# A two-layer trunk in float32: the residual stream kept feature-major instead of token-major

## The chip, the cores and the metric

One core of one Trainium2 chip runs the whole kernel in one launch. The metric is the device time of that launch in microseconds, median of three runs. Before the change they are 2691.78, 2687.07 and 2688.96 us, so the median is 2688.96 us.

## The reference, cut to what matters

The input is x (1024 tokens x 1024 features) with a conditioning vector c. Two layers, each a mixer and a feed-forward (hidden 2816), each wrapped the same way:

```
def rms_norm(x, g):
    y = x * lax.rsqrt(jnp.mean(x * x, axis=-1, keepdims=True) + EPS)
    return y * g
def modulate(h, shift, scale):
    return h * (1.0 + scale[:, None, :]) + shift[:, None, :]
...
    for layer in range(DEPTH):
        mod = silu(c) @ ada_w[layer] + ada_b[layer]
        sh1, sc1, g1, sh2, sc2, g2 = jnp.split(mod, 6, axis=-1)
        h = modulate(rms_norm(x, ln_mix_g[layer]), sh1, sc1)
        mix = even_mixer(h, ...) if layer % 2 == 0 else odd_mixer(h, ...)
        x = x + g1[:, None, :] * mix
        h = modulate(rms_norm(x, ln_ffn_g[layer]), sh2, sc2)
        x = x + g2[:, None, :] * swiglu(h, ffn_w_in[layer], ffn_w_out[layer])
```

The even mixer is chunked attention (A) beside a state space model (S5, whose input is u, a quarter of the input projection); the odd mixer is retention (C) beside stick-breaking attention (D). The statistics of the norm go over the features of one token; shift, scale and gate are one number for each feature.

## The kernel before, in words

T is 1024 tokens in NT = 8 tiles of 128, D is 1024 features in NK = 8 tiles of 128, the hidden layer is NH = 22 tiles taken in 11 blocks of FB = 2. Every float32 operand of a large product is split into two parts (hi and lo), and a product is three matmuls (mm3, L236 to L238). The weights come as one stream of units: a DMA into a raw tile, a copy to hi on ScalarE (L129), a subtraction to lo on GpSimd (L130; during the projections of A on VectorE). These whl and wo splits run ahead of their use.

The normalized, modulated activations stand feature-major in HT (feature on the partition, token along the row), as hi and lo. The residual x is token-major: x[t] holds 128 tokens. `rstd` squares a token tile on ScalarE with a running sum (L311) and takes the power -1/2 on GpSimd (L312 to L314); `norm` scales the rows on VectorE (xn, L323), turns eight 128x128 pieces on TensorE (L331), modulates on ScalarE (L334), and splits on VectorE (L336, L337).

In `out_proj` and in `ffn`'s outp the activations (HT, or aT, the gated hidden layer) are the stationary operand, the weights move, and a result is 128 tokens x 512 features in PSUM (banks mm, at and av). VectorE multiplies it by the gate (L1223, L1293), which has to lie along the row: so adaLN's parts 2 and 5 are broadcast over the partitions by a matmul with ones (L290) and a DMA of ada_b. GpSimd then adds the product into x (L1224, L1294); in the last block of a feed-forward VectorE adds. Other adaLN parts become columns by eight one-column matmuls (L297).

`first` starts the program: x comes in by tiles, `sums` on VectorE makes adaLN's weighted sums for the shift and scale of feature tile k (L368 to L371, eight per tile), `cols` reduces them to columns on TensorE (L378), `turn` transposes and normalizes at once by a matmul against a diagonal (dg, L407; L388), and the u projection (192 matmuls of 512 columns, five of eight token phases beside the loop) runs as feature tiles come in. After it the projections of A begin (a_dense, matmuls of 256 columns).

The order on each engine is set by a list scheduler on a simulated timeline, within what the code's steps (pipe.tick) allow: generators such as norm and ada give out a part at each step. Engines take their rows in order; a row whose input is late holds all rows behind it on its engine.

Of the kernel before, what the change touches and what calls it, by code (L numbers as in the profile page):

```python
# [30 lines left out]
class Split:  # L31
    """A float32 operand as the exact sum of two float32r parts."""
# [8 lines left out]
class Pipe:  # L41
    """Issues pieces of work in steps: a piece is a generator that yields how many steps to wait for its next part."""
# [25 lines left out]
class Unit:  # L68
    """One slot of the weight stream: [P, n] of a source, split on chip."""
# [20 lines left out]
class Stream:  # L90
    """All weights in the order of their use: loads run ahead, then the split into float32r parts."""
# [66 lines left out]
class Trunk:  # L158
    def __init__(self, ctx, tc, I, out):
# [16 lines left out]
        for name, shape in (("mixd", [NK, P, T]), ("cad", [P, 16, 2, P]), ("m2d", [P, 16, 2, P]), ("ed", [P, 16, 2, P]),  # L176
                            ("m1d", [P, 32, P]), ("kd", [16, 32, 16, 16]), ("ytd", [4, P, T]), ("vd", [8, P, NT, 64]),
                            ("qkd", [4, 2, 2, P, T]), ("xd", [T, D]), ("ud", [8, P, 512])):
            setattr(self, name, self.dr.tile(shape, F32, name=name))
        self.r8 = self.const.tile([P, 16], F32, name="r8")  # L180
        self.col, self.gbc, self.state, self.pp = {}, {}, None, None
# [4 lines left out]
    def plan(self):  # L186
        """the weights in the order of their use"""
# [52 lines left out]
    def project(self, ps, w, n, cols, ks=range(NK)):  # L240
        """token-major projection of the token columns cols, feature tiles ks"""
# [63 lines left out]
    def rstd(self, pool, xs):  # L305
        """1 / rms over the columns of the views xs [P, 4, P]"""
        nc = self.nc
        ss = self.sm.tile([P, 4], F32, tag="ss", bufs=4, name="ss")
        for h, x in enumerate(xs):
            f = pool.tile([P, 4, P], F32, tag="hf", bufs=2, name="hf")  # L310
            nc.scalar.activation(f, x, AF.Square, accum_out=ss[:, h:h + 1])  # L311
        nc.gpsimd.tensor_add(ss[:, 2:3], ss[:, 0:1], ss[:, 1:2])  # L312
        nc.gpsimd.tensor_scalar(ss[:, 2:3], ss[:, 2:3], 1.0 / D, EPS, M, A)
        nc.gpsimd.tensor_tensor(ss[:, 3:4], ss[:, 2:3], self.mhalf, ALU.pow)  # L314
        return ss[:, 3:4]

    def norm(self, pool, xt, t, sb):
        nc = self.nc
        s, b = (self.col[z] for z in sb)
        r = self.rstd(pool, [xt[:, h * 512:h * 512 + 512].rearrange("p (a b) -> p a b", a=4) for h in range(2)])  # L320
        yield 1
        xn = pool.tile([P, D], F32, tag="ada", bufs=1, name="xn")
        nc.vector.tensor_scalar(xn, xt, r, None, M)  # L323
        yield 1
        tok = slice(t * P, (t + 1) * P)
        for h in range(2):
            ps = self.at_bank()
            f = pool.tile([P, 4, P], F32, tag="hf", bufs=2, name="hf")
            for j in range(4):
                k = 4 * h + j  # L330
                nc.tensor.transpose(ps[:, j * P:(j + 1) * P], xn[:, k * P:(k + 1) * P], self.ident)  # L331
            for j in range(4):
                k = 4 * h + j
                nc.scalar.activation(f[:, j], ps[:, j * P:(j + 1) * P], AF.Identity, bias=b[:, k:k + 1], scale=s[:, k:k + 1])  # L334
            hi = self.HT.hi[:, 4 * h:4 * h + 4, tok]
            nc.vector.tensor_copy(hi, f)  # L336
            nc.vector.tensor_sub(self.HT.lo[:, 4 * h:4 * h + 4, tok], f, hi.bitcast(F32))  # L337

# [1 line left out]
    def first(self, keep, xp):  # L340
        """norm, modulation and the projection of u, feature tile by feature tile as adaLN's columns come in;
        ud[b][c, g, (s h')] = u of the groups 4 b + g at token 8 c + s"""
        nc, I, v, pipe = self.nc, self.I, self.nc.vector, self.pipe
        U = xp.tile([P, 32, 8, 16], F32, name="U")
        xs = xp.tile([P, NT, NK, P], F32, name="xs")
        dg = xp.tile([P, NT, P], F32, name="dg")
        uf = U.rearrange("p g s h -> p (g s h)")
        ax = xp.tile([P, 2048], F32, name="ax")
        slot = lambda k: ax if k % 3 == 2 else uf[:, k % 3 * 2048:k % 3 * 2048 + 2048]
# [9 lines left out]
        def sums(k):  # L359
            acc[k] = xp.tile([P, 2, P], F32, tag="ada0", bufs=2, name="ada0")  # L360
            ao = xp.tile([P, 4, P], F32, tag="hf", bufs=2, name="hf").rearrange("p a b -> p (a b)")[:, :256]
            two = acc[k].rearrange("p a b -> p (a b)"), ao
            for j in range(8):
                w = slot(k)[:, j * 256:j * 256 + 256]
                sc = self.sc[:, j:j + 1]
                a = two[j % 2]
                if j < 2:
# [3 lines left out]
            v.tensor_add(two[0], two[0], ao)  # L371
            if k + 3 < NK:
                load(k + 3)

        def cols(k):
            ps = self.av_bank()
            for j in range(2):
                nc.tensor.matmul(ps[:, j:j + 1], acc[k][:, j], self.ones[:, 0:1], start=True, stop=True)  # L378
# [3 lines left out]
            v.scalar_tensor_tensor(s, s, 1.0, self.lng[:, 0, 0, k:k + 1], A, M)  # L382

        def turn(k):
            for half in range(2):
                ps = self.at_bank()
# [11 lines left out]
        for t in range(NT):  # L398
            nc.sync.dma_start(out=xs[:, t], in_=I["x"][t * P:(t + 1) * P].rearrange("p (k f) -> p k f", k=NK))
# [1110 lines left out]
```

## Time and profile before

| | |
|---|---|
| runs | 2691.78, 2687.07, 2688.96 us |
| span of the profiled execution | 2688.1 us |
| TensorE busy | 2601.1 us (97%) |
| VectorE, ScalarE, GpSimd busy | 1162.3, 751.1, 1295.9 us |
| HBM traffic | 100 GB/s over the span |

The profiled execution has no time of its own beside its span; the span lies between the lowest and the highest run, 0.9 us below their median. PE is TensorE, DVE VectorE, ACT ScalarE, POOL GpSimd. PEclk is the granted TensorE clock as a share of full speed. In the rows, mm<-HT,whl means: moving operand HT, stationary operand whl, result in a bank called mm.

### The profile page before, as it was taken

What the parts mean: (1) busy time and instruction counts of PE and PEld (TensorE: products, weight loads), DVE (VectorE), ACT (ScalarE), POOL (GpSimd) and SP (SyncE); (2) the same over time, 40 slices, a digit from 0 to 9 for tenths busy, and PEclk for the clock granted to TensorE, in tenths of its full rate; (3) what the DMA queues carried; (4) which work ended last, traced back from release to release, by engine and by line L of the source; (5) the groups of instructions that cost most, each with busy time, mean ns of one, the idle gap of its engine ahead of it and who ended that gap; (6) DMA issues with size and microseconds to landing.
All of it is one profiled execution on the core that took longest, in us unless ns stands there. A gap on an engine that the chain in (4) does not pass through costs nothing. (4 is left out here: it accounts for less than half of the span.)

```text
span 2688.1 us, 33793 instructions
## 1 busy us (share of the span) xinstructions
PE 2601.1 (97%) x13008; PEld 2191.5 (82%) x13008; DVE 1162.3 (43%) x2169; ACT 751.1 (28%) x1496; POOL 1295.9 (48%) x975
## 2 busy tenths in 40 slices
PE   5999999999999999999999999999999999999999
PEld 5997788878887888888788888888778888888887
DVE  8477564374433332222521566666532222222224
ACT  3332567352111011111341444544431111111100
POOL 6365002655555576666422234423546555566654
PEclk8998989999999999999999999999999999999999
DMA  7277665434333221111244322214221111111101
GB/s 257 96 223 232 186 171 178 168 124 133 118 110 109 87 71 47 47 47 48 75 125 146 94 82 87 93 59 153 94 72 61 47 48 47 47 48 47 48 15 63
DMA packets 140448, 269.29 MB, mean 100 GB/s; under 512 B 33856, under 2 KB 73472, under 8 KB 139520
## 3 DMA queue, kind: packets, MB, share of 16 engines
q1 hardware_dynamic: 140288, 267.14, 30.6%
q8 instruction: 102, 1.67, 0.2%
q14 instruction: 58, 0.48, 0.1%
HBM read 223.32 MB, written 45.88 MB: 100 GB/s over the span
## 5 line engine op out<-in xcount | busy, mean ns | idle before, releaser
L238 PE MATMUL mm<-HT,whl 128*128 128x512 f32 x1536 | 604.3, 393 | 0.0
L236 PE MATMUL mm<-HT,whl 128*128 128x512 f32 x1536 | 601.0, 391 | 1.8 <-ACT sg L1276 1.8
L237 PE MATMUL mm<-HT,whl 128*128 128x512 f32 x1536 | 602.4, 392 | 0.0
L130 POOL TENSOR_TENSOR whl<-raw,whl 128x1024 fp32r<-128x1024 f32 x142 | 353.6, 2498 | 513.8 <-ACT whl L129 500.2
L1294 POOL TENSOR_TENSOR x<-x,tmp 128x512 f32<-128x512 f32 x320 | 409.8, 1296 | 92.0 <-DVE tmp L1293 84.4
L1293 DVE TENSOR_TENSOR tmp<-at,gate 128x512 f32<-128x512 f32 x352 | 242.7, 690 | 307.1 <-PE at L238 209.8
L236 PEld LDWEIGHTS mm<-HT,whl 128*128 128x128 f32 x1536 | 288.8, 188 | 66.3 <-ACT sg L1276 2.2
L237 PEld LDWEIGHTS mm<-HT,whl 128*128 128x128 f32 x1536 | 288.7, 188 | 66.0 <-issue 0.5
L238 PEld LDWEIGHTS mm<-HT,whl 128*128 128x128 f32 x1536 | 288.9, 188 | 60.0
L236 PE MATMUL mm<-whl,HT 128*128 128x512 f32 (+1 forms) x896 | 334.7, 374 | 2.3 <-ACT qk L513 2.3
L237 PE MATMUL mm<-whl,HT 128*128 128x512 f32 (+1 forms) x896 | 332.1, 371 | 0.0
L238 PE MATMUL mm<-whl,HT 128*128 128x512 f32 (+1 forms) x896 | 328.6, 370 | 0.0
L1277 DVE TENSOR_TENSOR sg<-sg,mm 128x512 f32<-128x512 f32 x88 | 60.4, 687 | 610.9 <-PE mm L238 607.8
L1276 ACT ACTIVATE sg<-mm 128x512 f32<-128x512 f32 x88 | 52.8, 600 | 947.2 <-PE mm L238 943.8
L236 PE MATMUL at<-wo,aT 128*128 128x512 f32 x704 | 276.1, 392 | 3.2 <-DVE tmp L1293 3.1
L237 PE MATMUL at<-wo,aT 128*128 128x512 f32 x704 | 275.7, 392 | 0.0
L238 PE MATMUL at<-wo,aT 128*128 128x512 f32 x704 | 274.4, 390 | 0.0
L129 ACT CAST whl<-raw 128x1024 fp32r<-128x1024 f32 x154 | 161.6, 1053 | 243.1 <-PE mm L238 200.5
L1279 POOL TENSOR_TENSOR aT<-sg,aT 128x512 fp32r<-128x512 f32 x88 | 115.3, 1310 | 223.2 <-DVE aT L1278 223.2
L236 PEld LDWEIGHTS mm<-whl,HT 128*128 128x128 f32 x896 | 178.6, 199 | 27.3 <-ACT qk L513 2.5
L237 PEld LDWEIGHTS mm<-whl,HT 128*128 128x128 f32 x896 | 178.6, 199 | 24.5 <-issue 0.2
L238 PEld LDWEIGHTS mm<-whl,HT 128*128 128x128 f32 x896 | 177.1, 199 | 24.8
(291 smaller groups left out, 3531.9 us busy)
## 6 DMA issues: line engine op xcount, KB each, us to landing
raw<-in_ffn_w_in SPq DMA_DIRECT2D x88, 512.0 KB, 3.5
raw<-in_ada_w SPq DMA_DIRECT2D x80, 512.0 KB, 4.0
raw<-in_ffn_w_out SPq DMA_DIRECT2D x44, 512.0 KB, 3.2
qkd<-stk SPq DMA_DIRECT2D x32, 256.0 KB, 4.7
q<-qkd SPq DMA_DIRECT2D x32, 256.0 KB, 4.7
ks<-qkd SPq DMA_DIRECT2D x32, 256.0 KB, 5.4
qkd<-stk SPq DMA_DIRECT2D x16, 512.0 KB, 3.0
raw<-in_cd_w_in_c SPq DMA_DIRECT2D x16, 512.0 KB, 4.2
```

What stands on the lines that cost most here:

```text
L129: nc.scalar.copy(hi, u.raw[:, :u.n])
L130: self.low.tensor_sub(lo, u.raw[:, :u.n], hi.bitcast(F32))
L236: mm(out, lhs.hi, rhs.hi, start=start, stop=False)
L237: mm(out, lhs.hi, rhs.lo, start=False, stop=False)
L238: mm(out, lhs.lo, rhs.hi, start=False, stop=stop)
L1276: nc.scalar.activation(sg, gu[0], AF.Silu)
L1277: nc.vector.tensor_mul(sg, sg, gu[1])
L1279: nc.gpsimd.tensor_sub(a[m].lo[:, sl], sg, a[m].hi[:, sl].bitcast(F32))
L1293: nc.vector.tensor_mul(tmp, ps, g2[:, sl])
L1294: add(x[t][:, sl], x[t][:, sl], tmp)
```

## The change

The residual becomes feature-major: x[n] holds features 128 n to 128 n + 127 of all tokens, x and the result are transposed on the host, and xd in DRAM follows. A gate and an rms scale change places: the gate is now a column, the scale lies along the row. So:

- in `out_proj` and outp the weights are stationary and HT or aT moves; VectorE evacuates with one instruction, x + gate column * PSUM (L1235, L1311), and GpSimd's add goes. Gates become columns like the other parts.
- `stat` squares each new half tile on ScalarE and GpSimd adds it to acc (L300). `rms` sums over the partitions with four one-column matmuls (L307), then VectorE (L309), GpSimd's power (L310), four diagonals on VectorE (L314), and one matmul with ones that puts the scale of 512 tokens along all rows of a bank, rb (L317). `norm` then works on 512 tokens: for each feature tile VectorE x * s * rb (L328), ScalarE + b into HT's hi (L330), VectorE the lo (L331). No transposes.
- in `first` the sum of squares goes over feature tiles, x is scaled in place by eight VectorE products (L416), turn reads x from SBUF, and adaLN's sums of even k are taken by TensorE (16 one-column matmuls, L375); odd k stay on VectorE.
- the last block of a feed-forward goes by token halves, the norm of a half starts with the half's last tile; four tiles of D's values (v_tile) stand behind it, four within d_dense. The stream's steps (pump, tick) sit elsewhere in `half`.

The diff, without docstrings and comments, cut to its core:

```diff
-        gate = part in (2, 5)
-        if gate:
-            acc = self.const.tile([P, D], F32, tag="gate", bufs=2, name="gate")
-        else:
-            acc = pool.tile([P, D], F32, tag="ada", bufs=1, name="ada")
+        acc = pool.tile([P, D], F32, tag="ada", bufs=1, name="ada")
         for k in range(NK + 1):
...
             yield 1
-        if gate:
-            bb = self.raw()
-            nc.sync.dma_start(out=bb, in_=self.I["ada_b"][layer, part * D:(part + 1) * D].partition_broadcast(P))
-            yield 2
-            for h in range(2):
-                ps = self.at_bank()
-                sl = slice(h * 512, h * 512 + 512)
-                nc.tensor.matmul(ps, self.ones, acc[:, sl], start=True, stop=True)
-                v.tensor_add(acc[:, sl], ps, bb[:, sl])
-            self.gbc[layer, part] = acc
-            return
...
+    def stat(self, pool, xt, n, h):
+        nc = self.nc
+        sl = slice(h * 512, h * 512 + 512)
+        if n == 0:
+            self.acc[h] = pool.tile([P, 512], F32, tag="acc", bufs=2, name="acc")
+            nc.scalar.activation(self.acc[h], xt[:, sl], AF.Square)
+            return
+        sq = pool.tile([P, 512], F32, tag="hf", bufs=2, name="hf")
+        nc.scalar.activation(sq, xt[:, sl], AF.Square)
+        nc.gpsimd.tensor_add(self.acc[h], self.acc[h], sq)
+    def rms(self, pool, acc):
+        nc, v, g = self.nc, self.nc.vector, self.nc.gpsimd
+        ps = self.at_bank()
+        for j in range(4):
+            nc.tensor.matmul(ps[:, j:j + 1], acc[:, j * P:(j + 1) * P], self.ones[:, 0:1], start=True, stop=True)
+        ss = self.sm.tile([P, 2, 4], F32, tag="ss", bufs=2, name="ss")
+        v.tensor_scalar(ss[:, 0], ps[:, :4], 1.0 / D, EPS, M, A)
+        g.tensor_tensor(ss[:, 1], ss[:, 0], self.mhalf.to_broadcast([P, 4]), ALU.pow)
+        yield 1
+        dg = pool.tile([P, 4, P], F32, tag="dgt", bufs=1, name="dgt")
+        for j in range(4):
+            v.tensor_scalar(dg[:, j], self.ident, ss[:, 1, j:j + 1], None, M)
+        yield 1
+        self.rb = self.at_bank()
+        nc.tensor.matmul(self.rb, self.ones, dg.rearrange("p a b -> p (a b)"), start=True, stop=True)
+    def norm(self, pool, x, h, sb):
         nc = self.nc
         s, b = (self.col[z] for z in sb)
...
+        yield from self.rms(pool, self.acc.pop(h))
+        rb = self.rb
+        yield 1
+        sl = slice(h * 512, h * 512 + 512)
+        for k in range(NK):
+            f = pool.tile([P, 512], F32, tag="nf", bufs=2, name="nf")
+            nc.vector.scalar_tensor_tensor(f, x[k][:, sl], s[:, k:k + 1], rb, M, M)
+            hi = self.HT.hi[:, k, sl]
+            nc.scalar.activation(hi, f, AF.Identity, bias=b[:, k:k + 1])
+            nc.vector.scalar_tensor_tensor(self.HT.lo[:, k, sl], f, b[:, k:k + 1], hi.bitcast(F32), A, S)
+            if k % 2:
+                yield 1
...
-            ao = xp.tile([P, 4, P], F32, tag="hf", bufs=2, name="hf").rearrange("p a b -> p (a b)")[:, :256]
-            two = acc[k].rearrange("p a b -> p (a b)"), ao
+            a = acc[k].rearrange("p a b -> p (a b)")
             for j in range(8):
...
                 sc = self.sc[:, j:j + 1]
-                a = two[j % 2]
-                if j < 2:
+                if j == 0:
                     v.tensor_scalar(a, w, sc, None, M)
...
                     v.scalar_tensor_tensor(a, w, sc, a, M, A)
-            v.tensor_add(two[0], two[0], ao)
-            if k + 3 < NK:
-                load(k + 3)
         def cols(k):
...
             for j in range(2):
-                nc.tensor.matmul(ps[:, j:j + 1], acc[k][:, j], self.ones[:, 0:1], start=True, stop=True)
+                if k % 2:
+                    nc.tensor.matmul(ps[:, j:j + 1], acc[k][:, j], self.ones[:, 0:1], start=True, stop=True)
+                    continue
+                for i in range(8):
+                    c0 = i * 256 + j * P
+                    nc.tensor.matmul(ps[:, j:j + 1], slot(k)[:, c0:c0 + P], self.sc[:, i:i + 1], start=i == 0, stop=i == 7)
             for j in range(2):
...
             v.scalar_tensor_tensor(s, s, 1.0, self.lng[:, 0, 0, k:k + 1], A, M)
+            if k + 3 < NK:
+                load(k + 3)
         def turn(k):
             for half in range(2):
-                ps = self.at_bank()
-                for t in range(4):
-                    nc.tensor.matmul(ps[:, t * P:(t + 1) * P], xs[:, 4 * half + t, k], dg[:, 4 * half + t], start=True, stop=True)
+                sl = slice(half * 512, half * 512 + 512)
                 f = xp.tile([P, 512], F32, tag="tf", bufs=3, name="tf")
-                nc.scalar.activation(f, ps, AF.Identity, bias=cs[:, 1, k:k + 1], scale=cs[:, 0, k:k + 1])
-                sl = slice(half * 512, half * 512 + 512)
+                nc.scalar.activation(f, xs[:, k, sl], AF.Identity, bias=cs[:, 1, k:k + 1], scale=cs[:, 0, k:k + 1])
                 (v.tensor_copy, nc.scalar.copy)[half](self.HT.hi[:, k, sl], f)
...
         load(0)
-        for t in range(NT):
-            nc.sync.dma_start(out=xs[:, t], in_=I["x"][t * P:(t + 1) * P].rearrange("p (k f) -> p k f", k=NK))
+        for k in range(NK):
+            nc.sync.dma_start(out=xs[:, k], in_=I["x"][k])
         self.stream.dma()
...
         load(2)
-        sums(0)
-        for t in range(NT):
-            r = self.rstd(xp, [xs[:, t, 4 * h:4 * h + 4] for h in range(2)])
-            v.tensor_scalar(dg[:, t], self.ident, r, None, M)
+        ac = xp.tile([P, T], F32, name="xacc")
+        for k in range(NK):
+            if k == 0:
+                nc.scalar.activation(ac, xs[:, 0], AF.Square)
+                continue
+            for half in range(2):
+                sl = slice(half * 512, half * 512 + 512)
+                sq = xp.tile([P, 512], F32, tag="tf", bufs=3, name="sq")
+                nc.scalar.activation(sq, xs[:, k, sl], AF.Square)
+                v.tensor_add(ac[:, sl], ac[:, sl], sq)
+        for half in range(2):
+            sl = slice(half * 512, half * 512 + 512)
+            for _ in self.rms(xp, ac[:, sl]):
+                pass
+            nc.scalar.copy(rbs[:, sl], self.rb)
+        for k in range(NK):
+            v.tensor_mul(xs[:, k], xs[:, k], rbs)
+            if k == 0:
+                sums(1)
         pipe.tick()
...
                 cols(n)
-            if n + 1 < NK:
-                sums(n + 1)
             if n < NK:
                 turn(n)
+            if n % 2 == 0 and n + 3 < NK:
+                sums(n + 3)
             if n > 1:
...
-                self.mm3(ps, self.HT[:, k, t * P:(t + 1) * P], w[n].k(k), k == order[0], k == order[-1])
-        def evac(n, t, ps):
-            sl = slice(n * 512, n * 512 + 512)
-            tmp = pool.tile([P, 512], F32, tag="otmp", bufs=2, name="otmp")
-            nc.vector.tensor_mul(tmp, ps, g1[:, sl])
-            nc.gpsimd.tensor_add(x[t][:, sl], x[t][:, sl], tmp)
+                self.mm3(ps, w[n // 4].k(k)[:, n % 4 * P:n % 4 * P + P], self.HT[:, k, h * 512:h * 512 + 512],
+                         k == order[0], k == order[-1])
+        def evac(n, h, ps):
+            xh = x[n][:, h * 512:h * 512 + 512]
+            nc.vector.scalar_tensor_tensor(xh, ps, self.col[layer, 2][:, n:n + 1], xh, M, A)
+            self.stat(pool, x[n], n, h)
+        first = [(0, 0), (1, 0), (2, 0), (3, 0), (0, 1), (1, 1)]
...
-        for n, t in [(0, 6), (0, 7)] + [(1, t) for t in range(NT)]:
+        for n, h in [(2, 1), (3, 1)] + [(n, h) for h in range(2) for n in range(4, 8)]:
             ps = self.mm_bank()
-            part(n, t, ps, order)
-            evac(n, t, ps)
-            if n == 0 and t == 6:
-                pipe.tick()
-            elif n == 0:
+            part(n, h, ps, order[:4])
+            pipe.tick()
+            part(n, h, ps, order[4:])
+            evac(n, h, ps)
+            if (n, h) == (3, 1):
                 w[0].free()
                 pipe.tick(*extra)
+            elif n == 7:
+                if h:
+                    w[1].free()
+                pipe.tick(self.norm(pool, x, h, sb))
             else:
-                pipe.tick(self.norm(pool, x[t], t, sb))
-        w[1].free()
-    def ffn(self, pool, layer, x, put, store, extra=()):
+                pipe.tick()
...
-                    self.stream.pump()
+                    if u == 0:
+                        pipe.tick()
...
+            def outp(ms, h, after=lambda n, h: None):
+                sl = slice(h * 512, h * 512 + 512)
+                for n in range(NK):
                     ps = self.at_bank()
-                    sl = slice(n * 512, n * 512 + 512)
                     for m in ms:
-                        self.mm3(ps, a[m][:, tok], wfo[m].k(0)[:, sl], m == ms[0], m == ms[-1])
-                    tmp = pool.tile([P, 512], F32, tag="otmp", bufs=2, name="tmp")
-                    nc.vector.tensor_mul(tmp, ps, g2[:, sl])
-                    add(x[t][:, sl], x[t][:, sl], tmp)
-                    done(t, sl)
+                        self.mm3(ps, wfo[m].k(0)[:, n * P:(n + 1) * P], a[m][:, sl], m == ms[0], m == ms[-1])
+                    xh = x[n][:, sl]
+                    nc.vector.scalar_tensor_tensor(xh, ps, self.col[layer, 5][:, n:n + 1], xh, M, A)
+                    after(n, h)
+                    if n % 4 == 3:
+                        if n == NK - 1 and h:
+                            for m in ms:
+                                wfo[m].free()
+                        pipe.tick()
...
+                last = bi + 1 == len(blocks)
+                if bi == 0:
+                    inp(ms + blocks[1][:1])
+                elif not last:
                     inp(ms[1:])
...
+                    inp(blocks[bi + 1][:1])
                 else:
...
+                    start(ms[1])
+                for h in range(2):
+                    if last:
+                        half(ms[1], h)
+                    outp(ms, h, *([done] if last else []))
...
+        def done(n, h):
+            if h:
+                nc.sync.dma_start(out=k.xd[n], in_=x[n])
+            k.stat(xp, x[n], n, h)
+            if n == NK - 1:
+                pipe.start(k.norm(xp, x, h, [(1, 1), (1, 0)]))
+        k.ffn(xp, 0, x, done, [lambda l=l, p=p: k.ada(xp, l, p) for l, p in ((1, 1), (1, 0), (1, 2), (1, 4), (1, 3))])
+        for t in range(4):
+            pipe.tick(k.v_tile(xp, "nf", k.wdv, t))
+            pipe.tick()
+        pipe.drain()
...
-                for t in (NT - 2, NT - 1):
+                for t in range(4, NT):
...
-    I["x"] = c(a["x"].reshape(T, D))
+    I["x"] = c(a["x"].reshape(T, D).T.reshape(NK, P, T))
...
-_OUTS = [((1, T, D), "float32")]
+_OUTS = [((NK, P, T), "float32")]
```

What this does to the order. First TensorE at the program's start, down to the first matmuls of the u projection (L236, L237). Before:

```order
1 L378 MATMUL av<-ones,ada_152 128x1 x2
2 L388 MATMUL at<-dg,xs 128x128 x24
3 L236 MATMUL mm<-whl,HT 128x512
4 L237 MATMUL mm<-whl,HT 128x512
5 L236 MATMUL mm<-whl,HT 128x512
```

And now:

```order
1 L375 MATMUL av<-scond,U 128x1 x16
2 L307 MATMUL at<-ones,xacc 128x1 x4
3 L317 MATMUL at<-dgt,ones 128x512
4 L307 MATMUL at<-ones,xacc 128x1 x4
5 L371 MATMUL av<-ones,ada_229 128x1 x2
6 L375 MATMUL av<-scond,ax 128x1 x11
7 L317 MATMUL at<-dgt,ones 128x512
8 L375 MATMUL av<-scond,ax 128x1 x5
9 L371 MATMUL av<-ones,ada_275 128x1 x2
10 L236 MATMUL mm<-whl,HT 128x512
11 L237 MATMUL mm<-whl,HT 128x512
```

Before, the first u matmul followed the transposes of three feature tiles; now both halves' rms matmuls stand ahead of it. On VectorE, eight products over the whole of x stand ahead of the first split of HT (L388):

```order
161 L783 TENSOR_TENSOR pts<-rn,rq 128x16
162 L416 TENSOR_TENSOR xs<-xs,rbs 128x1024 x8
163 L781 TENSOR_TENSOR rn<-pts 128x16
164 L782 TENSOR_TENSOR rq<-pts 128x16
165 L784 SCALAR_TENSOR_TENSOR pts<-pts 128x16
166 L377 TENSOR_TENSOR col_109<-av,adab 128x1 x2
167 L388 CAST HT<-tf 128x512 x2
```

Before, VectorE's cast of a feature tile needed only that tile's columns and its turn; now the eight products come between. On GpSimd at the same place the weights' splits stand between the powers:

```order
13 L130 TENSOR_TENSOR whl<-raw,whl 128x1024
14 L310 TENSOR_TENSOR ss<-ss,mhalf 128x4
15 L130 TENSOR_TENSOR whl<-raw,whl 128x1024
16 L310 TENSOR_TENSOR ss<-ss,mhalf 128x4
17 L130 TENSOR_TENSOR whl<-raw,whl 128x1024 x4
18 L389 TENSOR_TENSOR HT<-tf,HT 128x512 x16
```

A power thus waits for a split, and four splits follow the second power. Last, TensorE near the end of layer 0's feed-forward, where the norm of the first token half begins (now):

```order
5066 L237 MATMUL mm<-HT,whl 128x512
5067 L238 MATMUL mm<-HT,whl 128x512
5068 L307 MATMUL at<-ones,acc 128x1 x4
5069 L317 MATMUL at<-dgt,ones 128x512
5070 L236 MATMUL at<-aT,wo 128x512
5071 L237 MATMUL at<-aT,wo 128x512
```

The broadcast L317 stands right behind the columns L307 on which it depends by way of VectorE and GpSimd, with no other TensorE work between; in `out_proj` 29 to 37 matmuls stand between the two.

## Rows read from the trace of the kernel before

**Rows 1.** page, part 1: busy time, share of the span, instructions.

```profile
PE 2601.1 (97%) x13008; PEld 2191.5 (82%) x13008; DVE 1162.3 (43%) x2169; ACT 751.1 (28%) x1496; POOL 1295.9 (48%) x975
```

**Rows 2.** windows; stretch, its length, busy of each engine, PEclk, DMA share, GB/s.

```profile
10.00:83.00 73.00, 55.74 (x236) 50.32 (x237) 69.75 (x235) 30.16 (x59) 43.07 (x45) 0.84 0.61 223
...
500.00:640.00 140.00, 136.92 (x629) 110.99 (x628) 85.35 (x90) 51.03 (x115) 74.99 (x60) 1.00 0.43 146
640.00:1300.00 660.00, 656.92 (x2894) 539.07 (x2894) 213.39 (x281) 85.46 (x99) 399.51 (x260) 1.00 0.23 77
...
1860.00:2000.00 140.00, 133.39 (x612) 107.88 (x611) 68.38 (x83) 49.61 (x115) 60.66 (x57) 0.99 0.29 103
```

**Rows 3.** PE's waits: for what, us in total, times, longest.

```profile
PE av L378 <- DVE ada L371: 20.1, 4, 10.7
PE at L331 <- DVE xn L323: 9.9, 6, 3.1
...
PE at L236 <- DVE tmp L1293: 3.1, 2, 2.5
...
PE mm L236 <- ACT sg L1276: 1.8, 1, 1.8
```

**Rows 4.** groups by line: busy, mean ns of one, idle before, releasers.

```profile
L1293 DVE TENSOR_TENSOR tmp<-at,gate 128x512 f32<-128x512 f32 x352 | 242.7, 690 | 307.1 <-PE at L238 209.8 <-POOL x L1294 97.3
...
L331 PE MATMUL at<-ident,xn 128*128 128x128 f32 x192 | 25.8, 277 | 10.0 <-DVE xn L323 9.9
...
L297 PE MATMUL at<-ones,ada 128*128 128x1 f32 x96 | 11.0, 245 | 0.0
...
L290 PE MATMUL at<-gate,ones 128*128 128x512 f32 x16 | 7.5, 592 | 0.0
```

**Rows 5.** timeline of PE after a wait; start, us, instruction.

```profile
1972.72 1.51 PE L331 MATMUL at<-ident,xn 128*128 128x128 f32 x8 [3.13 <-DVE xn L323]
...
1975.30 0.63 PE L236 MATMUL mm<-HT,whl 128*128 128x512 f32 x1
...
1976.58 0.44 PE L236 MATMUL mm<-HT,whl 128*128 128x512 f32 x1
```

**Rows 6.** timeline of POOL and DVE, at 19, 22 and 1957 us.

```profile
19.52 1.28 POOL L393 TENSOR_TENSOR HT<-tf,HT 128x512 fp32r<-128x512 f32 x1
19.53 1.35 DVE L407 TENSOR_SCALAR dg<-ident,ss 128x128 f32<-128x128 f32 x1
...
21.83 0.20 POOL L312 TENSOR_TENSOR ss<-ss 128x1 f32<-128x1 f32 x1
...
22.93 2.41 POOL L130 TENSOR_TENSOR whl<-raw,whl 128x1024 fp32r<-128x1024 f32 x1
23.07 2.30 DVE L691 SCALAR_TENSOR_TENSOR sn<-sn,rz 128x16 f32<-128x16 f32 x1
...
1955.08 4.96 POOL L130 TENSOR_TENSOR whl<-raw,whl 128x1024 fp32r<-128x1024 f32 x2
...
1957.80 2.79 DVE L337 TENSOR_TENSOR HT<-hf,HT 128x512 fp32r<-128x512 f32 x1
```

**Rows 7.** groups by line, operations like the added ones.

```profile
L531 POOL TENSOR_TENSOR ass<-ass,mhalf 128x8 f32<-128x8 f32 x16 | 29.5, 1847 | 0.8
...
L314 POOL TENSOR_TENSOR ss<-ss,mhalf 128x1 f32<-128x1 f32 x32 | 20.9, 653 | 2.4
...
L370 DVE SCALAR_TENSOR_TENSOR hf<-U,scond,hf 128x256 f32<-128x256 f32 x18 | 11.7, 651 | 0.0
...
L610 DVE TENSOR_TENSOR HT<-raw,HT 128x1024 fp32r<-128x1024 f32 x6 | 8.2, 1359 | 1.7 <-ACT HT L609 1.7
```

**Rows 8.** timeline of PE: first u matmul, last one, a_dense's first.

```profile
28.91 0.78 PE L236 MATMUL mm<-whl,HT 128*128 128x512 f32 x1
...
109.70 0.40 PE L238 MATMUL mm<-whl,HT 128*128 128x512 f32 x1
109.94 0.28 PE L236 MATMUL mm<-whl,HT 128*128 128x256 f32 x1
```

More of the change, by code (lines that the diff above doesn't have):

```diff
@@ L1212, in out_proj, with part @@
         nc, pipe = self.nc, self.pipe
-        g1 = self.gbc[layer, 2]
         w = self.wout[layer]
-        def part(n, t, ps, ks):
+        order = list(order)
+        def part(n, h, ps, ks):
             for k in ks:
-                self.mm3(ps, self.HT[:, k, t * P:(t + 1) * P], w[n].k(k), k == order[0], k == order[-1])
-        def evac(n, t, ps):
-            sl = slice(n * 512, n * 512 + 512)
-            tmp = pool.tile([P, 512], F32, tag="otmp", bufs=2, name="otmp")
-            nc.vector.tensor_mul(tmp, ps, g1[:, sl])
-            nc.gpsimd.tensor_add(x[t][:, sl], x[t][:, sl], tmp)
+                self.mm3(ps, w[n // 4].k(k)[:, n % 4 * P:n % 4 * P + P], self.HT[:, k, h * 512:h * 512 + 512],
+                         k == order[0], k == order[-1])
@@ L1226, in out_proj @@
+        def evac(n, h, ps):
[3 more added lines that the diff above has]
+        first = [(0, 0), (1, 0), (2, 0), (3, 0), (0, 1), (1, 1)]
         banks = [self.mm_bank() for _ in range(3)] + [self.at_bank() for _ in range(2)] + [self.av_bank()]
         for k in order[:-late]:
-            for t, ps in enumerate(banks):
-                part(0, t, ps, [k])
+            for (n, h), ps in zip(first, banks):
+                part(n, h, ps, [k])
@@ L1230, in out_proj @@
             pipe.tick()
-        for t, ps in enumerate(banks):
-            part(0, t, ps, order[-late:])
-            evac(0, t, ps)
+        for (n, h), ps in zip(first, banks):
+            part(n, h, ps, order[-late:])
+            evac(n, h, ps)
             pipe.tick()
-        for n, t in [(0, 6), (0, 7)] + [(1, t) for t in range(NT)]:
+        for n, h in [(2, 1), (3, 1)] + [(n, h) for h in range(2) for n in range(4, 8)]:
             ps = self.mm_bank()
-            part(n, t, ps, order)
-            evac(n, t, ps)
-            if n == 0 and t == 6:
-                pipe.tick()
-            elif n == 0:
+            part(n, h, ps, order[:4])
+            pipe.tick()
+            part(n, h, ps, order[4:])
+            evac(n, h, ps)
+            if (n, h) == (3, 1):
@@ L1257, in inp @@
                 for m in ms:
-                    aT = fp.tile([P, 2, T], F32R, tag="aT", bufs=FB + 1, name="aT")
-                    a[m] = Split(aT[:, 0], aT[:, 1])
+                    start(m)
                 for h in range(2):
@@ L1262, in inp, with start @@
                         half(m, h)
-                        pipe.tick()
+            def start(m):
+                aT = fp.tile([P, 2, T], F32R, tag="aT", bufs=FB + 1, name="aT")
+                a[m] = Split(aT[:, 0], aT[:, 1])
             def half(m, h):
@@ L1358, in build @@
     with tc.tile_pool(name="xp0", bufs=1, reuse_waits="tile") as xp:
-        x = [xp.tile([P, D], F32, name=f"x{t}") for t in range(NT)]
-        for t in range(NT):
-            nc.sync.dma_start(out=x[t], in_=I["x"][t * P:(t + 1) * P])
+        x = [xp.tile([P, T], F32, name=f"x{n}") for n in range(NK)]
+        for n in range(NK):
+            nc.sync.dma_start(out=x[n], in_=I["x"][n])
         pipe.start(k.ada(xp, 0, 3))
         k.out_proj(xp, 0, x, [0, 1, 2, 4, 5, 6, 7, 3], 5, [(0, 4), (0, 3)], [k.ada(xp, 0, 5)])
-        def put(t, sl):
-            if sl.stop == D:
-                nc.sync.dma_start(out=k.xd[t * P:(t + 1) * P], in_=x[t])
-        def store(t, done=[]):
-            if t is not None:
-                pipe.tick(k.norm(xp, x[t], t, [(1, 1), (1, 0)]))
-            else:
-                pipe.tick()
-            done.append(t)
-            u = len(done) - 4
-            if u >= 0:
-                pipe.tick(k.v_tile(xp, "otmp", k.wdv, u))
-            if t is None:
-                pipe.drain()
-        k.ffn(xp, 0, x, put, store, [lambda l=l, p=p: k.ada(xp, l, p) for l, p in ((1, 1), (1, 0), (1, 2), (1, 4), (1, 3))])
+        def done(n, h):
[7 more added lines that the diff above has]
+            pipe.tick(k.v_tile(xp, "nf", k.wdv, t))
+            pipe.tick()
+        pipe.drain()
     with tc.tile_pool(name="dense1", bufs=1, reuse_waits="tile") as dp:
@@ L1397, in build @@
     with tc.tile_pool(name="xp1", bufs=1, reuse_waits="tile") as xp:
-        x = [xp.tile([P, D], F32, name=f"x{t}") for t in range(NT)]
+        x = [xp.tile([P, T], F32, name=f"x{n}") for n in range(NK)]
         for kk in (0, 1, 2, 4, 5, 6):
@@ L1401, in build @@
         pipe.tick(k.mix_split(3, 512))
-        for t in range(NT):
-            nc.sync.dma_start(out=x[t], in_=k.xd[t * P:(t + 1) * P])
+        for n in range(NK):
+            nc.sync.dma_start(out=x[n], in_=k.xd[n])
         pipe.tick()
```

70 lines of the change are left out of this document (9 added, 61 removed).

## The prediction

> **What bounds the kernel.** The page's first part says that TensorE is busy 97% of the span [rows 1], so first comes the table of windows, to see where the other 3% lie. In the middle of the feed-forward TensorE has 656.92 of 660 us while GpSimd has 399.51 and VectorE 213.39 [rows 2]: there neither a cheaper evacuation nor a lighter GpSimd moves the end. VectorE's evacuation L1293 waited 97.3 us for GpSimd's add, yet the two matmul waits on it come to 3.1 us [rows 3, 4]. Time can be won only by taking matmuls away, or where TensorE waits: the two ends of the out projection (136.92 of 140 and 133.39 of 140) and the program's start, where VectorE is the full engine (69.75 of 73 us, TensorE 55.74 at a granted clock of 0.84) [rows 2]. There TensorE waits 20.1 us for VectorE's adaLN sums [rows 3]. The waits give the second list: transposes for xn 9.9 us in 6, feed-forward results for tmp 3.1, for sg 1.8 [rows 3].
>
> **TensorE's work, from these rows.** All is counted against the profiled execution, 2688.1 us, since it has no time beside its span; the runs' median lies 0.9 us above, inside their scatter.
> Removed: 24 groups of eight transposes, 25.8 us busy, so 1.07 each [rows 4], of which about 0.2 overlaps the next matmul (an estimate): 24 x 0.87 = -21. Four gates' broadcasts: -7.5 [rows 4].
> Added: the columns of six parts cost 11.0 us, 1.83 a part [rows 4]; four gates more, +7.3. Six norms of a half outside the start: four columns (half a part, 0.92) and one broadcast (7.5 / 8 = 0.94), 6 x 1.86 = +11.2.
> Net -10. The products themselves are as many as before, only with operands exchanged; I count nothing for it. Bounds from both sides: 0.01 us in each of 2880 matmuls would be 29 us either way, but out projection and feed-forward have both roles in the program before and both run without gaps in the middle stretch [rows 2], so I keep 4 us either way.
>
> **Waits that go.** With the transposes go their 9.9 us; the tmp wait of 3.1 goes with GpSimd's add (a single evacuation has no second step to wait for); 1.8 at sg goes since the norm's splits no longer stand in its way there: -14.8. After the longest of them matmuls start 1.28 us apart for three, 0.43 each [rows 5], the lower of the two clock levels (1.2 GHz), against 0.23 at 2.4; seven such, twice, are -2.8. Together about -17.6, so the sure part of the change is -27.6. What takes the place of these waits decides the sign.
>
> **End of layer 0's feed-forward.** L317 stands right behind L307 on TensorE, so VectorE's L309, GpSimd's power, four diagonals and the hand-overs between them lie open. The power on 128x4 lies between 0.65 (128x1) and 1.85 (128x8) [rows 7], I take 1.1; with four diagonals of about 0.28 and three hand-overs, 3.1 us. It can be longer: a split of 2.4 us stands ahead of the power in GpSimd's rows and another right behind it, and VectorE steps are held while GpSimd runs one: an operation of 128x16 took 2.30 us beside a split of 2.41, a diagonal 1.35 us beside a subtraction of 1.28, HT's lo part 2.79 [rows 6]. The two add 4.9, so 3.1 to 8.0. Behind TensorE's waiting row stand the out products of the first half, and nobody else is ready. I take 5.4, plus 1.4 for matmuls at the lower clock, plus 2.7 for the second half, whose L317 has three matmuls (0.7 us) in front: +9.5, bounds 5 and 14.
> A rule of the Trainium skill bears on this ("SBUF — State Buffer", "Who interferes with whom"): a VectorE instruction with one SBUF input outside its two-port modes does not contend with GpSimd, one with two inputs does, and whoever issues first keeps the shared ports to its end. A diagonal has one SBUF input; read by the first half of the rule it would go free and this end would cost 5, but the row of 1.35 shows one held, so the two-port half of the rule applies and the middle value stands. The same rule speaks against the new lo step and the eight products in the start, which read two SBUF operands.
>
> **Ends of the out projection (two).** 29 to 37 matmuls, 7 us and more, cover L307 to L317. Then HT's half has to be made: eight times L328 (PSUM and SBUF, like L1293: 0.69 [rows 4]), ScalarE, and L331, which is like the row of 2.79 when held and some 0.7 when not. The first feed-forward matmuls take feature tile after feature tile at 3 x 0.23 = 0.7 us, VectorE makes one in 1.4: the last two tiles come late. Free of holding the rest of the out projection hides it (0); with two or three tiles held 2 us each it is 3 to 5 at each end, plus one L317 behind adaLN's sums in layer 0. +9 for both, bounds 0 and 14. GpSimd's adds into acc and ScalarE's squares are hidden by products of the same stretch; without that cover a last add of 1.3 would show, inside the bounds.
>
> **The start.** VectorE loses four of eight tiles' sums (8 x 0.65 = 5.2 each [rows 7], 21 us) and eight diagonals, and gains 14 adds and eight products of 128x1024 at 1.36 [rows 7], 10.9. But the order changes from tile by tile to all at once: no u matmul before all of x is squared, the scale known twice and x multiplied. Squares done at 21.8 [rows 6]; two rms steps of 4 to 5 us, partly beside each other, 8; sums of tile 1, 5.2 (3.8 unheld); some 36 small operations of 0.17 in between in VectorE's order, 6; the products 10.9; turn, cast and lo of the first tile, 2.3. That is about 53, less 2 where they overlap: 51 unheld. GpSimd's six splits of 2.4 each hold VectorE once, at most 14.4: 65. Middle 58, where before it was 28.91 [rows 8]. From then on TensorE has 192 matmuls of 0.247 (0.24 in the last step [rows 8]), 47.4; columns of two even tiles, each 16 at 0.23, 7.3; the rest of the odd ones and a cold beginning, 4: 59. The first matmul of A's projections then starts at 110 to 124, middle 117, against 109.94 [rows 8]: +7, bounds 0 and 15. So the gap ahead of the u projection eats what the earlier waits for sums gave.
>
> **Sum.** 2688.1 - 27.6 + 9.5 + 9 + 7 = 2686.0. The likeliest case, that what goes and what comes almost cancel, has its own range from 2676 to 2697.
>
> **Rivals.**
> B. The new waits are mostly hidden: VectorE issues first or splits have run by then. Start 110 (-7), end of the feed-forward 5 (-4.5), ends of the out projection 3 (-6): 2668.5. For it: VectorE works only 85.35 of 140 us around the out projection [rows 2], so there is room, and the stream runs ahead. Against: L317's place behind L307 gives 3 us away even unheld.
> C. Slower: one mechanism, GpSimd's weight splits holding VectorE's two-input steps. Its place is the start, ahead of the u projection, and again each norm. Price: u begins at 66, A's projections at 125 (+8 over the middle), the feed-forward's end 14 (+4.5), the out projection 14 (+5): 2703.5. It decides from the point where the three losses pass 34 us, so with stage ends at their middle (18.5) from a start that is 15 us late, with both at their top (28) from 6. For it: every held row above. Against: fewer subtractions and no adds into x leave GpSimd freer, and splits that come early hold nothing of weight.
> D. The change does not free VectorE in the start at all, if TensorE's 16 columns a tile wait for the adaLN loads: the loads of tile k + 3 are now issued only behind the columns of tile k. It would show as C does, and is counted there.
>
> **Chances.** Cancel 0.46 (faster 0.16, same 0.26, slower 0.04), B 0.27 (faster 0.25, same 0.02), C with D 0.27 (slower 0.26, same 0.01). About 0.2% (5.4 us) is what a measurement of this kernel can tell from no change: faster 0.41, same 0.29, slower 0.30. The range reaches to B's and C's values, 2667 to 2708.
>
> **What will show it.** Right: no GpSimd add behind outp, a middle of the feed-forward as full as before; A's first 256-column matmul between 110 and 124; a gap of 3 to 8 us at L317 in layer 0's feed-forward end, released by VectorE's dgt; small gaps at the first feed-forward matmuls, released by HT. The start's term is wrong if u begins before 48 or after 66. The whole is wrong if the middle of the feed-forward gets gaps, or if a matmul with the weights stationary takes another time than the same with them moving: 0.005 us each would be 14 us.

## The result and the profile after

The changed kernel takes 2714.36 us (median of four, 2706.66 to 2719.08) against 2690.37 us; ratio 1.0085, 95% interval 1.0063 to 1.0106. It is slower, and outside the range forecast. Its profiled execution (span 2704.5 us) is the fastest of its four, 16.4 us over that of the kernel before; the medians lie 24.0 us apart.

First the page's first part of the changed kernel, answering to [rows 1]:

```profile
PE 2606.3 (96%) x12928; PEld 2183.3 (81%) x12928; DVE 1145.3 (42%) x2123; ACT 712.7 (26%) x1289; POOL 875.0 (32%) x577
```

GpSimd lost 421 us of work, and TensorE has 80 records fewer but is busy 5 us longer. Next the windows of the changed kernel (columns as in [rows 2]): the start, the middle of layer 0's feed-forward, layer 1's out projection, and 100 us of layer 1's feed-forward.

```profile
10.00:83.00 73.00, 38.74 (x166) 35.26 (x166) 65.59 (x192) 27.01 (x38) 35.89 (x19) 1.00 0.61 223
...
640.00:1300.00 660.00, 660.00 (x2889) 536.63 (x2889) 206.65 (x277) 84.75 (x99) 194.16 (x99) 1.00 0.23 74
...
1885.00:2035.00 150.00, 150.00 (x661) 120.83 (x660) 64.09 (x85) 42.50 (x56) 67.59 (x39) 1.00 0.28 96
...
2100.00:2200.00 100.00, 100.00 (x434) 81.19 (x433) 29.62 (x42) 12.25 (x14) 28.75 (x15) 1.00 0.15 51
```

The same 100 us of the kernel before:

```profile
2100.00:2200.00 100.00, 100.00 (x439) 82.16 (x438) 24.99 (x37) 12.85 (x15) 63.10 (x43) 1.00 0.12 43
```

Here is most of the loss: TensorE is full in both, at full clock, but issues 434 matmuls where it issued 439. The busy share cannot show that; the count in an equal stretch does. The first and last of 98 matmuls of the feed-forward's input product before, (2221.85 - 2199.65) / 97 = 0.2289 us apart:

```profile
2199.65 0.39 PE L237 MATMUL mm<-HT,whl 128*128 128x512 f32 x1
...
2221.85 0.40 PE L238 MATMUL mm<-HT,whl 128*128 128x512 f32 x1
```

and of 109 after, 25.20 / 108 = 0.2333 us apart:

```profile
2199.69 0.40 PE L238 MATMUL mm<-HT,whl 128*128 128x512 f32 x1
...
2224.89 0.40 PE L238 MATMUL mm<-HT,whl 128*128 128x512 f32 x1
```

These matmuls (HT moving, whl stationary) are the same before and after. There are 2 layers x 22 tiles x 2 halves x 2 x 24 = 4224 of them; times 0.0044 us that is 18.6 us, more than the 16.4 between the profiles and most of the 24.0 between the medians. The waits of TensorE after, as in [rows 3]:

```profile
PE at L317 <- DVE dgt L314: 19.2, 5, 7.4
PE av L371 <- DVE col L377: 15.3, 1, 15.3
PE at L307 <- DVE xacc L409: 8.5, 1, 8.5
PE av L375 <- DMA U<-in_ada: 7.0, 1, 7.0
...
PE at L307 <- POOL acc L300: 3.2, 1, 3.2
```

The waits for xn, tmp and sg are gone; new are those of the start (the second and third row, and 9.9 of the first's 19.2), of layer 0's feed-forward's end (7.4 of the first, 6.0 of it for the first token half) and of layer 0's out projection (1.8, and the last row). The fourth row is the first matmul of the program; it is the only wait of L375 for an adaLN load, so rival D did not come.

What moved the input product? No instruction of it changed, but the two gate tiles of 4096 bytes left the constant pool and four columns of 32 came. HT lies ahead of them, at byte 2208 of each partition in both programs as compiled; all tiles behind moved down by 8064 bytes. The lowest whl tile went from byte 93280 to 85216, and the others stand whole multiples of 512 from it. The distance whl minus HT, stationary minus moving operand, modulo 512 (the rest after division by 512), went from 448 to 64.

Marks of the profiled executions, in us:

| | before | after |
|---|---|---|
| first u matmul | 28.91 | 64.20 |
| A's projections | 109.94 | 123.45 |
| layer 0's out projection | 484.99 | 487.65 |
| layer 0's first out product (outp) | 657.47 | 665.63 |
| C's projections, 336 matmuls in a row | 1396.26 | 1416.01 |
| layer 1's out projection, its row of 48 matmuls into at | 1872.84 | 1892.68 |
| layer 1's first outp | 2024.57 | 2033.16 |

### The profile page after: what moved, and what is told of

Its sections match the earlier page's. It is cut to its first block, busy times and chain, and to the rows that moved or that the text cites. A ratio compares the mean times of both kernels' runs of the same rounds, so it can differ in the third digit from the quotient of the medians.

```text
span 2704.5 us, 32586 instructions
## 1 busy us (share of the span) xinstructions
PE 2606.3 (96%) x12928; PEld 2183.3 (81%) x12928; DVE 1145.3 (42%) x2123; ACT 712.7 (26%) x1289; POOL 875.0 (32%) x577
## 4 chain that ended last, share of the span: by engine, by line
PE 84%; DVE 6%; DMA 5%; issue 1%; POOL 1%; ACT 1%; SPq 0%; DVEq 0%; ACTq 0%; POOLq 0%
PE mm L236 18%; PE mm L237 18%; PE mm L238 18%; PE at L236 6%; PE at L238 6%; PE at L237 6%; PE av L507 3%; DMA raw<-in_ada_w 2%; PE at L498 2%; PE at L486 1%; DVE ada L276 1%; DVE w L1164 1%; PE mm L486 1%; DMA e<-ed 1%; PE at L282 0%
## 5 line engine op out<-in xcount | busy, mean ns | idle before, releaser
L237 PE MATMUL mm<-HT,whl 128*128 128x512 f32 x1744 | 690.3, 396 | 1.3 <-DVE HT L331 1.3
L236 PE MATMUL mm<-HT,whl 128*128 128x512 f32 x1744 | 690.8, 397 | 0.5 <-ACT HT L330 0.5
L238 PE MATMUL mm<-HT,whl 128*128 128x512 f32 x1744 | 690.7, 396 | 0.0
L237 PEld LDWEIGHTS mm<-HT,whl 128*128 128x128 f32 x1744 | 328.5, 188 | 80.8 <-DVE HT L331 2.0
L236 PEld LDWEIGHTS mm<-HT,whl 128*128 128x128 f32 x1744 | 328.5, 188 | 79.7 <-ACT HT L330 0.9
L238 PEld LDWEIGHTS mm<-HT,whl 128*128 128x128 f32 x1744 | 328.5, 188 | 78.8 <-issue 0.2
L1311 DVE SCALAR_TENSOR_TENSOR x<-at,col,x 128x512 f32<-128x512 f32 x352 | 262.7, 751 | 276.5 <-PE at L238 276.4
L236 PE MATMUL at<-aT,wo 128*128 128x512 f32 x704 | 276.7, 396 | 0.0
L238 PE MATMUL at<-aT,wo 128*128 128x512 f32 x704 | 276.4, 393 | 0.0
L237 PE MATMUL at<-aT,wo 128*128 128x512 f32 x704 | 274.7, 390 | 0.0
L236 PE MATMUL mm<-whl,HT 128*128 128x512 f32 (+1 forms) x688 | 249.5, 363 | 4.4 <-ACT ve L455 3.1
L130 POOL TENSOR_TENSOR wo<-raw,wo 128x1024 fp32r<-128x1024 f32 x44 | 104.7, 2398 | 442.8 <-ACT wo L129 442.8
L237 PE MATMUL mm<-whl,HT 128*128 128x512 f32 (+1 forms) x688 | 247.1, 359 | 0.0
L238 PE MATMUL mm<-whl,HT 128*128 128x512 f32 (+1 forms) x688 | 244.6, 358 | 0.0
L129 ACT CAST wo<-raw 128x1024 fp32r<-128x1024 f32 x44 | 44.2, 1046 | 501.1 <-PE at L238 491.6
L238 PEld LDWEIGHTS at<-aT,wo 128*128 128x128 f32 x704 | 132.5, 188 | 29.9
L237 PEld LDWEIGHTS at<-aT,wo 128*128 128x128 f32 x704 | 132.7, 188 | 29.6 <-issue 0.5
```

The source lines that it names most:

```text
L129: nc.scalar.copy(hi, u.raw[:, :u.n])
L130: self.low.tensor_sub(lo, u.raw[:, :u.n], hi.bitcast(F32))
L236: mm(out, lhs.hi, rhs.hi, start=start, stop=False)
L237: mm(out, lhs.hi, rhs.lo, start=False, stop=False)
L238: mm(out, lhs.lo, rhs.hi, start=False, stop=stop)
L1311: nc.vector.scalar_tensor_tensor(xh, ps, self.col[layer, 5][:, n:n + 1], xh, M, A)
```

## The experiments

Distance between the operands. Seven kernels that keep the order of every engine; only unused bytes or the places of tiles differ:

```diff
 a_whl384, a_whl192, a_d0, a_d128 (96, 48, 112, 16 floats; changed kernel)
+        self.pad = self.const.tile([P, 96], F32, name="pad")    # behind HT
 a_both384: the same 96 floats ahead of HT
 b_ht384, b_ht192: adab (384 bytes), or r8 and lng (192), allocated ahead of HT (kernel before)
```

> The changed kernel with 384 unused bytes per partition allocated behind HT, so that every tile behind it (raw, whl, x, aT, wo) lies 384 bytes further and HT stays; the weights then stand to HT as in the kernel before (whl minus HT is 448 modulo 512 bytes, as before; 64 in the changed kernel). The order on every engine is the changed kernel's. Theory 1, the place of the stationary whl tile relative to the moving HT sets the interval of the feed-forward's first matmuls: interval 0.2289 us as before instead of 0.2335, 4224 such matmuls, so about 19 us less than the changed kernel, span 2685. Rival, the new order or the steps in half slow them: 0.2335 and a span of 2704 as it is.

> The changed kernel with the same 384 bytes ahead of HT: HT and whl both move, their distance stays. Theory 1 (relative place): interval 0.2335, span 2704, no gain. Rival, the absolute place of whl (224 modulo 256 bytes, here 96 as before): 0.2289 and span 2685. Rival, the order: 2704 too.

> The changed kernel with 192 bytes behind HT: whl minus HT is 256 modulo 512 bytes. Theory 1 with a period of 256 bytes: like wo and aT (distance 0), so 0.228 and span about 2681; with a period of 512 bytes unknown, between 0.228 and 0.236. The order as a cause: 0.2335, span 2704.

> The kernel before with one small constant tile of 384 bytes allocated ahead of HT instead of behind it: HT moves 384 bytes up, whl and all else stay, whl minus HT becomes 64 modulo 512 as in the changed kernel. The order is unchanged. Theory 1: the feed-forward's first matmuls slow from 0.2289 to 0.2335, span about 2688 + 19 = 2707, less some us where the weights move and HT is stationary. Rivals (order, absolute place of whl): 2688 as it is.

> The kernel before with two small constant tiles of 192 bytes together allocated ahead of HT, so that whl minus HT is 256 modulo 512 bytes as in the variant of the changed kernel with 192 bytes. Order unchanged. Theory of distance: feed-forward's first matmuls at 0.2268 instead of 0.2289, -9 us; 256-column matmuls at 0.120 instead of 0.114, +4: span 2683. Then at equal distance the change itself is worth 2675 minus this number.

> The changed kernel with 448 unused bytes behind HT: whl minus HT is 0 modulo 512 bytes. By the theory of distance the interval of the feed-forward's first matmuls is again another one; like wo and aT, whose distance is 0, it should be 0.228 or less, span near 2683. If distance is not the cause it stays at 0.2335.

> The changed kernel with 64 unused bytes behind HT: whl minus HT is 128 modulo 512 bytes. No value forecast from a row; between those of 64 (0.2335) and 256 (0.2268), so about 0.231 and a span near 2694, if the interval falls evenly with distance.

Measured (interval of the feed-forward's input product in us; ratio to the kernel before run beside each; a_d128 has two runs, the others four to ten):

| kernel | whl - HT mod 512 | interval | median us | ratio, 95% |
|---|---|---|---|---|
| before | 448 | 0.2289 | 2688.6 to 2690.6 | 1 |
| a_whl384 | 448 | 0.2289 | 2693.51 | 1.0025 (1.0005, 1.0045) |
| after | 64 | 0.2333 | 2714.36 | 1.0085 (1.0063, 1.0106) |
| a_both384 | 64 | 0.2333 | 2711.01 | 1.0092 (1.0062, 1.0122) |
| b_ht384 | 64 | 0.2333 | 2700.20 | 1.0048 (1.0027, 1.0068) |
| a_whl192 | 256 | 0.2267 | 2675.99 | 0.9954 (0.9936, 0.9973) |
| b_ht192 | 256 | 0.227 | 2675.68 | 0.9952 (0.9938, 0.9967) |
| a_d0 | 0 | 0.2267 | 2680.77 | 0.9966 (0.9950, 0.9982) |
| a_d128 | 128 | 0.2324 | 2715.62 | 1.0104 (1.0079, 1.0129) |

The pair that tells the distance from the place: a_whl384 (111 matmuls, 25.18 / 110 = 0.2289) and a_both384 (109, 0.2333). Their whl tiles lie at the same bytes (85600 the lowest), only HT differs:

```profile
2199.72 0.39 PE L236 MATMUL mm<-HT,whl 128*128 128x512 f32 x1
...
2224.90 0.39 PE L238 MATMUL mm<-HT,whl 128*128 128x512 f32 x1
```

```profile
2199.61 0.39 PE L236 MATMUL mm<-HT,whl 128*128 128x512 f32 x1
...
2224.81 0.39 PE L236 MATMUL mm<-HT,whl 128*128 128x512 f32 x1
```

The same matmul in the changed kernel with 192 bytes (timeline; 62 matmuls, 13.83 / 61 = 0.2267):

```profile
2199.73 0.39 PE L237 MATMUL mm<-HT,whl 128*128 128x512 f32 x1
...
2213.56 0.40 PE L238 MATMUL mm<-HT,whl 128*128 128x512 f32 x1
```

and in the kernel before with HT moved by 384 bytes (109 matmuls, 25.20 / 108 = 0.2333), its order untouched:

```profile
2199.60 0.40 PE L238 MATMUL mm<-HT,whl 128*128 128x512 f32 x1
...
2224.80 0.40 PE L238 MATMUL mm<-HT,whl 128*128 128x512 f32 x1
```

The interval follows the distance and nothing else that was varied: moving both tiles changes nothing; moving whl alone (changed kernel) or HT alone (kernel before) does. That shows the cause. The sign counts too. In layer 1's out projection of the kernel before HT is stationary and whl moves, so stationary minus moving is 64 there, and 127 matmuls stand 29.40 / 126 = 0.2333 us apart, in the same execution whose feed-forward has 0.2289:

```profile
1884.82 0.40 PE L236 MATMUL mm<-whl,HT 128*128 128x512 f32 x1
...
1914.22 0.40 PE L236 MATMUL mm<-whl,HT 128*128 128x512 f32 x1
```

In b_ht384 the two change places: its out projection has 0.2289 (127 matmuls from 1893.85 to 1922.69), its feed-forward 0.2333. That is part of why it loses 11.6 us in the medians (2700.20 against 2688.61) and not the 19 expected.

My guess for a_d128 failed (0.231 expected, 0.2324 found, and 2715.62 in place of 2694): the interval does not fall evenly. 0 and 256 act alike, which fits a period of 256 bytes; no other pair tests it. Which resource the two reads meet in is not shown. At equal distance the change is worth +0.25% at 448, nothing at 256 (2675.99 against 2675.68).

The start.

```diff
-        for k in range(NK):
-            v.tensor_mul(xs[:, k], xs[:, k], rbs)
...
-                nc.scalar.activation(f, xs[:, k, sl], AF.Identity, bias=..., scale=cs[:, 0, k:k + 1])
+                v.scalar_tensor_tensor(f, xs[:, k, sl], cs[:, 0, k:k + 1], rbs[:, sl], M, M)
+                nc.scalar.activation(f, f, AF.Identity, bias=cs[:, 1, k:k + 1])
```

> The changed kernel, only its start altered: the eight products of x and rms over 128x1024 are gone; instead each turn multiplies its 128x512 half by the scale column and the rms row in one VectorE instruction (ScalarE then adds the bias). Theory 1, the products that all stand ahead of the first u matmul set the start: u begins at about 55 us instead of 64, the projections of A at 115 instead of 123; if the stages behind keep that, span 2696. Rival, the two rms steps and GpSimd's splits set it: u stays at 62 to 64. Second rival, attention absorbs whatever the start gives (of 13.5 us lost at A's projections 2.7 were left at the out projection): A's projections at 115, out projection within 2 us of 488, span 2704.

Median 2702.69 us, 11.7 under the changed kernel (the intervals of the two ratios to the kernel before just touch: 1.0036 to 1.0070 and 1.0063 to 1.0106). In its timeline u begins and A's projections follow 9.3 and 7.6 us earlier, as the first theory had it:

```profile
54.95 0.78 PE L236 MATMUL mm<-whl,HT 128*128 128x512 f32 x1
...
115.89 0.28 PE L236 MATMUL mm<-whl,HT 128*128 128x256 f32 x1
```

Does attention absorb it? Its out projection begins at 484.25. The changed kernel's own mark, 487.65, is no good witness: a_gap3, a_gap3b and the five padded variants of the changed kernel, all with the same start, have 491.37 to 499.29, this kernel and a_all2 484.25 and 484.50. So most of the gain stays, and the 2.7 us left at 487.65 came from one early execution. The second rival falls. The same early execution makes every span that I forecast from the changed kernel's 2704.5 too low: a_whl384 2685 against 2692.6, a_turnwise 2696 against 2700.5, a_gap3b 2696 against 2705.7.

The end of layer 0's feed-forward, with one number, then without touching where the norm ends (the lines are those of every norm):

```diff
-        yield 1
+        yield 3        # in rms, ahead of the broadcast L317
 a_gap3b besides: no yield behind rms, and k % 3 == 2 for k % 2 in norm
```

> The changed kernel, only the step count ahead of the rms broadcast altered (3 in place of 1), so that in layer 0's feed-forward end 21 matmuls stand on TensorE between L307 and L317 where there was none, and some more for the second half. Theory: the wait of 7.4 us for VectorE's dgt in this end goes, and the matmuls at the lower clock behind it: 7 to 10 us less, span 2696. Rival, the norm behind it only comes later and TensorE waits for HT at the value tiles: no change, 2702 to 2706.

> As a_gap3, but the norm's later steps are drawn together so that its last write of HT comes as many steps after its start as in the changed kernel; 21 matmuls between L307 and L317 in layer 0's feed-forward end for the first half and 27 for the second. Theory: the wait of 7.4 us for dgt goes, with the slow clock behind it: 7 to 9 us less, span 2696. Rival: TensorE waits later for HT instead, in d_dense or the value tiles, and less than 3 us are won.

a_gap3 has 2702.36 us, but its norm is issued behind some products that read HT, so these read it without the norm's result and do not wait for it; it is only an upper bound on the gain. a_gap3b keeps that order and has 2706.62, 7.7 less than the changed kernel, but the intervals of the two ratios overlap (1.0047 to 1.0089 and 1.0063 to 1.0106), so the whole time alone does not show the gain. The stretch does: its waits hold no dgt from 1300 to 1420 us:

```profile
PE mm L236 <- ACT ve L455: 3.0, 1, 3.0
PE at L237 <- POOL aT L1298: 1.8, 1, 1.8
```

From the first out product to C's projections it needs 740.54 us, the changed kernel 750.38 (a_both384 and a_turnwise, which keep this end, 748.74 and 748.01). From there to the end the two need 1288.0 and 1288.5 us. So the theory holds for this stretch; the forecast span does not.

> The changed kernel with all three: 192 bytes behind HT, turn-wise products, 3 steps ahead of the broadcast. If the three effects add, 2675 - 8 - 8 = 2659; if attention absorbs the start, 2667.

> a_whl192, a_turnwise and a_gap3b in one. If they add: 2675 (a_whl192's span) - 4 (a_turnwise) - 8 = 2663. If the norm only moves, 2671.

a_all contains a_gap3 and its 2658.40 us fall under the same reserve. a_all2 has 2661.48 us, ratio 0.9899 (0.9877, 0.9921): the fastest version whose products wait for the norm, 1% under the kernel before, 14.5 under a_whl192 where the two effects alone came to 19.4. About half of that 1% is the distance: the kernel before with 192 bytes moved (b_ht192) has 2675.68.

## Why the prediction was wrong

The step that failed is the sentence on the products: "as many as before, only with operands exchanged; I count nothing for it", with 4 us as bounds. It measured +18.6 us (4224 x 0.0044), and in matmuls that I had not even in view, since nothing in them was exchanged. The exchanged ones came out as assumed: outp 0.228 on average before and 0.229 after (wo minus aT is 0 modulo 512 in both), layer 1's out projection 0.2333 before and after (after: 176 matmuls from 1904.66 to 1945.50). But for the out projection that was luck: the exchange alone turns the sign of the distance and gives 0.2289 (a_whl384, 176 matmuls from 1902.15 to 1942.21), worth 3.4 us if all 768 gain 0.0044, and the moved addresses took this away again. The reason given, that both roles run without gaps in the middle stretch, could not bear the term: the kernel before already had 0.2333 with HT stationary and 0.2289 with whl stationary, both in rows of matmuls without a gap. I looked for each edit's instructions, not for what a removed tile does to the addresses of those behind it. The closing part of the prediction named 0.005 us a matmul as what would overturn it, but gave it no chance.

TensorE's work and the waits that go: right in kind. Layer 1's out projection to its first outp, where no new wait came (150.00 of 150 us above), shrank from 151.73 to 140.48 us.

The start: u at 64.20 (51 to 65 forecast) and A's projections at 123.45 (110 to 124), the top of both ranges; middle +7, found +13.5. The reason given holds: a_turnwise, without the eight products ahead, has u at 54.95. The holding is larger than in the middle value: here VectorE's four diagonals take 5.07 us and, the other way round, one split takes 7.60 while the eight products run unheld (timelines of the changed kernel, VectorE and GpSimd):

```profile
38.90 5.07 DVE L314 TENSOR_SCALAR dgt<-ident,ss 128x128 f32<-128x128 f32 x4
...
50.46 9.18 DVE L416 TENSOR_TENSOR xs<-xs,rbs 128x1024 f32<-128x1024 f32 x8
```

```profile
54.25 7.60 POOL L130 TENSOR_TENSOR whl<-raw,whl 128x1024 fp32r<-128x1024 f32 x1 [10.77 <-ACT whl L129]
```

The end of the feed-forward: +9.5 forecast, bounds 5 and 14; 9.8 us came back from it in the profile of a_gap3b. The place and the chain were as said:

```profile
1329.41 0.95 PE L307 MATMUL at<-ones,acc 128*128 128x1 f32 x8
1336.36 2.08 PE L317 MATMUL at<-dgt,ones 128*128 128x512 f32 x2 [6.00 <-DVE dgt L314]
1337.44 1.42 PE L236 MATMUL at<-aT,wo 128*128 128x512 f32 x1
1338.65 0.63 PE L237 MATMUL at<-aT,wo 128*128 128x512 f32 x1
1339.08 0.63 PE L238 MATMUL at<-aT,wo 128*128 128x512 f32 x1
```

Inside the wait of 6.00 us the power stands behind a split and the four diagonals are held beside the next one (GpSimd, then VectorE):

```profile
1328.76 2.38 POOL L130 TENSOR_TENSOR whl<-raw,whl 128x1024 fp32r<-128x1024 f32 x1
1331.08 1.21 POOL L310 TENSOR_TENSOR ss<-ss,mhalf 128x4 f32<-128x4 f32 x1
1332.27 2.33 POOL L130 TENSOR_TENSOR whl<-raw,whl 128x1024 fp32r<-128x1024 f32 x1
...
1332.33 3.97 DVE L314 TENSOR_SCALAR dgt<-ident,ss 128x128 f32<-128x128 f32 x4 [0.91 <-POOL ss L310]
```

Then matmuls stand 0.43 apart, at a granted clock of 0.50, the lower level (1.2 GHz):

```profile
1337.40:1341.00 3.60, 3.60 (x9) 2.50 (x8) 2.40 (x4) 1.38 (x2) 0.00 (x0) 0.50 0.02 9
```

The out projections: layer 0 had 6.8 us of new waits (acc 3.2, dgt 1.8, HT 1.8) where I gave 4.5; layer 1 none. GpSimd's adds into acc, which I had hidden, show in layer 0.

Rival C's value (2703.5) lies close to the profiled 2704.5, but by accident: its holding was there and cost some us, the bulk was the distance. Without that (a_whl384) the change is 0.25% slower than before, about 5 us, where I forecast 2 less.

## What to carry to other kernels

Where TensorE is full, compare matmuls per stretch and the interval of one kind of matmul, not busy shares. Whenever a tile is added or removed ahead of matmul operands, look at where these now lie. Then try a few paddings between stationary and moving operand: here 192 unused bytes in the changed kernel are worth 1.4%, more than the whole restructure. A broadcast or column matmul needs other TensorE work between it and the one it depends on, and on VectorE no long row of work should stand ahead of the first thing that TensorE waits for.

## What the runs showed of the hardware

Unexpected: in these runs the interval of a 128x512 float32r matmul stream depends on the distance of its two SBUF operands, stationary minus moving: 0.2267 us at 0 and at 256 bytes, 0.2333 at 64, 0.2324 at 128, 0.2289 at 448, all modulo 512. And the holding between VectorE and GpSimd goes both ways: a split of 2.4 us, begun at 54.25 us among the eight products of two SBUF operands, lasted 7.60 and ended at 61.85, 2.2 us after the last product. The Trainium skill ("SBUF — State Buffer", "Who interferes with whom") says that whoever issues first keeps the shared ports for its whole instruction and the other is blocked. For these rows the trace agrees, and by these times the split stayed held from one product to the next.
